# First MLP, first four output tiles: contraction-outermost, between the tiles of the attention's output projection

## The chip, the cores and the metric

One core of one Trainium2 chip. The time is the device time of one execution in microseconds. The median of three runs of the kernel before is 1281.89 us (1281.35 to 1282.48).

## The reference

A trunk of two layers over 512 tokens of width 1024, all in float32. Each layer adds a token mixer, a squared-ReLU MLP and a gated embedding to x; every part starts from an RMS norm of x. The place of this case is the end of the first mixer and the beginning of the first MLP:

```python
x = x + dilated_window_mixer(rmsnorm(x, a_norm[j]), ...)   # ends with  o @ w_o
...
x = x + sq_relu_mlp(rmsnorm(x, mlp_norm[i]), w_up[i], w_down[i])
...
def sq_relu_mlp(h, w_up, w_down):
    return jnp.square(jax.nn.relu(h @ w_up)) @ w_down
```

`w_up` is 1024 x 4096, `w_down` 4096 x 1024.

## The kernel before

x lies transposed, features on the 128 partitions: eight tiles `x[0]` to `x[7]` of 128 features by 512 tokens. A product is float32 made of parts: every operand is split into a rounded high part and the rest (`split`, `fetch`), and `mm3` (L160) issues three matmuls, high by high, low by high and high by low. ACT makes a high part (L169, L172; L137 for weights), DVE the low part (L170, L173; L138 for weights).

The weights lie in one array in the order of `_schedule` (L43). `load` (L141) fetches a block and those ahead of it in that order: one DMA by SyncE (SP, L136), a cast on ACT, a subtraction on DVE. The pool `wp` has three slots each for the raw, high and low blocks of up to 128 x 1024.

`Norm` (L213) collects a norm while x is being made: `tile(m)` splits `x[m]` with the gain and adds its square to `acc` (ACT squares; the additions run on POOL by default and on the engine given to it otherwise, the last one always on DVE, L235). `columns` (L257) sums `acc` over the partitions by matmuls with ones, DVE works out the inverse root, and `row` (L210 and L264) spreads it over all partitions. The scale 1/rms goes on after the matmul (`up`, L640), so matmuls can start on unscaled tiles.

The first mixer's output projection has eight contraction tiles. Six of them (`woA1`) are woven into the last heads; the last two (`woA2`) come behind, one output tile at a time (L616): five matmuls, the residual sum `residual` (L284, DVE), `nM.tile(m)`. Then `mlp(0, nM)` begins: `up(0, b)` makes two hidden tiles by `dense` (L275), each with its eight contraction tiles in a row in one PSUM bank; behind the first come `columns` and, after the second, `row`; DVE and ACT then make relu, scale, square and split of the pair. There are four chunks of eight hidden tiles; `down` of a chunk adds into x. PSUM has eight banks (pool `pp`).

Within each engine the instructions run in the order that a scheduler gave them when the program was built; it keeps close to the order of the code and chooses the slots of the pools.

Of the kernel before, what the change touches and what calls it, by code (L numbers as in the profile page):

```python
# [23 lines left out]
P = 128  # L24
S = 512
D = 1024
KD = D // P
# [12 lines left out]
G_A, G_B, G_MLP, G_PLE, G_FIN, G_Q, G_KV, G_N = 0, 8, 16, 32, 48, 56, 58, 59  # L40


def _schedule():  # L43

    out = []
    for i in range(GH):
        out += [(("qkv", i, b), 1024) for b in range(4)]
        if i == 0:
            out += [(("v0", b), n * 320) for b, n in enumerate((3, 3, 2))]
    out += [(("woA1", m), 768) for m in range(8)]  # L50
    out += [(("woA2", h), 1024) for h in range(2)]
    out += _mlp_blocks(0)
    out += [(("win", b), 832) for b in range(4)]
    out += [((n, 0), c) for n, c in (("uq", 768), ("ukv", 512))]
    for g in range(1, 4):
        out += [((n, g), c) for n, c in (("uq", 768), ("ukv", 512))]
    out += [(("woB", h, b), 1024) for h in range(2) for b in range(4)]
    out += _mlp_blocks(1)
    return out


def _mlp_blocks(l):
    up = lambda c: [(("up", l, c, m), 1024) for m in range(8)]
    down = lambda c: [(("down", l, c, m), 1024) for m in range(8)]
    out = up(0)
    for c in range(NCH):
        if c + 1 < NCH:
            u = up(c + 1)
            out += u[:2] + down(c) + u[2:]
        else:  # L70
            out += down(c)
    out += [(("proj", l, h), 1024) for h in range(2)]
    out += [(("gate", l, m), 1024) for m in range(8)]
    return out
# [3 lines left out]
def trunk(ctx: ExitStack, tc: tile.TileContext, xT, pT, cols, mask, tabs, wts, out):  # L78
    nc = tc.nc
    V, A, G, T = nc.vector, nc.scalar, nc.gpsimd, nc.tensor  # L80
# [14 lines left out]
    def unit(dt=F32, shape=(P, 1024)):  # L95
        return ar.tile(list(shape), dt, tag="u", name=nm("u"))
# [515 lines left out]
        else:  # L612
            weave(attnA(i), woA1(), 48, 7)

    nM = Norm(G_MLP)
    for m in range(KD):  # L616
        ps = bank()
        w = load(("woA2", m // 4))
        c = m % 4 * 256
        mm3(ps, (w[0][:, c:c + P], w[1][:, c:c + P]), oA[4], True, False)  # L620
        T.matmul(ps, w[0][:, c + P:c + 256], oA[7][0], start=False, stop=False)
        T.matmul(ps, w[1][:, c + P:c + 256], oA[7][0], start=False, stop=True)
        residual(m, ps)
        nM.tile(m)


    def mlp(l, nM):
        rb = [None]

        def up(c, b):  # L630
            u = unit()
            ps = []
            for j in range(2):
                ps.append(dense(("up", l, c, 2 * b + j), KD, nM.k))
                if rb[0] is None and j == 0:
                    nM.columns()
            if rb[0] is None:
                rb[0] = nM.row()
            for j in range(2):
                V.scalar_tensor_tensor(u[:, j * S:(j + 1) * S], ps[j], 0.0, rb[0], op0=ALU.max, op1=ALU.mult)  # L640
            A.activation(u, u, AF.Square)
            h, lo = unit(F32R), unit(F32R)
            split(h, lo, u)
            return [(h[:, j * S:(j + 1) * S], lo[:, j * S:(j + 1) * S]) for j in range(2)]

        nG = Norm(G_PLE + 8 * l)
        hid = [up(0, b) for b in range(4)]
        for c in range(NCH):
            flat = sum(hid, [])
            if c == NCH - 1:  # L650
                preload(AF.Sigmoid)
                pr = unit()
                nc.sync.dma_start(out=pr, in_=pT[:, l * 1024:(l + 1) * 1024])
                pe = unit(F32R), unit(F32R)
                split(*pe, pr)
            nxt = []
            if c + 1 < NCH:
                nxt.append(up(c + 1, 0))
            for m in range(KD):
                residual(m, dense(("down", l, c, m), KD, lambda k: flat[k]))  # L660
                if c == NCH - 1:
                    nG.tile(m)
            if c + 1 < NCH:
                nxt += [up(c + 1, b) for b in range(1, 4)]
            hid = nxt
        return nG, pe
# [45 lines left out]
            add(m)  # L712
        return end

    nG, pe = mlp(0, nM)
    nB = Norm(G_B)
    lastA = gate(0, nG, pe, nB)

# [7 lines left out]
    for tp in range(2):  # L726
        ps = [bank(), bank()]
        for k in range(KD):
            w, c = load(("win", k // 2), 1 if tp else 0), (k % 2) * 416
# [19 lines left out]
    for j in range(2):  # L749
        ps = bank()  # L750
# [32 lines left out]
    pk, ps = bank(), bank()  # L783
# [189 lines left out]
    nM = Norm(G_MLP + 8)  # L973
    run(woB(1))
    nG, pe = mlp(1, nM)
# [3 lines left out]
    rb = None  # L979
# [56 lines left out]
    for h in range(2):  # L1036
# [3 lines left out]
        for b in range(4):  # L1040
            ps = [bank() for _ in range(2 if (h, b) == (1, 3) else 1)]
            for j in range(2):
                w = load(("gate", 1, 2 * b + j, h), 1)
# [23 lines left out]
def _arrange(inp):  # L1067
# [18 lines left out]
    def tiles(w, rows, cols_):  # L1086

        a = w[rows][:, cols_]
        return a.reshape(-1, P, a.shape[1]).transpose(1, 0, 2)
# [14 lines left out]
    def block(key):  # L1104
# [18 lines left out]
        if n == "ukv":  # L1123
            kv = ukv[:, key[1] * 512:(key[1] + 1) * 512].reshape(P, 4, 2, 64)
            return kv.transpose(0, 2, 1, 3)
        if n == "up":
            l, c, m = key[1:]
            return one(up[l], 0, 8 * c + m)
# [56 lines left out]
```

## Time and profile before

| | us |
|---|---|
| median of three runs | 1281.89 |
| lowest and highest | 1281.35, 1282.48 |
| the profiled execution's own time | 1284.43 |
| its span in the trace | 1282.6 |
| its mean granted clock of PE | 0.99 of full speed |

The span is the part of the execution that the trace covers. Durations in the rows come from the profiled execution. Starts on PE are the ones to read: a matmul's duration includes its way through the array, and the next one starts before it ends.

### The profile page before, as it was taken

Reading aid. Unit: us, or ns where it says so; the run is one execution under the profiler, and the core shown is the slowest. Engines: PE = TensorE matmul, PEld = TensorE weight load, DVE = VectorE, ACT = ScalarE, POOL = GpSimd, SP = SyncE. Lnnn points to the kernel's source line nnn. Section 1 sums busy time; section 2 is a strip of 40 time slices with the busy share of each in tenths; the row PEclk is TensorE's granted clock in tenths of the full one; section 3 lists DMA queues with packets and bytes.
Section 4 is the critical chain, followed back from the end, with each engine's and each line's share of the span. In section 5 each row is a group of like instructions: output and inputs, shape, how many; then the busy total and the mean of one; then the engine's idle time right before and its main releaser. Section 6 shows DMA issues by size and latency. Waiting matters only on the chain.

```text
span 1282.6 us, 16154 instructions
## 1 busy us (share of the span) xinstructions
PE 1252.5 (98%) x6224; PEld 1057.6 (82%) x6224; DVE 738.5 (58%) x1236; ACT 586.7 (46%) x967; POOL 147.8 (12%) x183
## 2 busy tenths in 40 slices
PE   8999999899999999999999999999999999999997
PEld 6888888688888888888888888888888888888896
DVE  6566676643343343454878999864434434335477
ACT  5566654532231331344558897754313313224464
POOL 5000000300000000021134443220000000000200
PEclk9999999899999999999998999999999999999998
DMA  6111122222222222232221010122232223223242
GB/s 224 66 66 66 58 71 101 68 99 97 92 92 97 99 99 99 99 115 89 81 62 38 17 51 17 50 82 84 98 99 99 99 99 99 98 91 109 98 157 106
DMA packets 34348, 113.18 MB, mean 88 GB/s; under 512 B 4064, under 2 KB 4832, under 8 KB 34272
## 3 DMA queue, kind: packets, MB, share of 16 engines
q1 hardware_dynamic: 34272, 112.15, 26.2%
q8 instruction: 49, 0.80, 0.3%
q14 instruction: 27, 0.22, 0.1%
HBM read 110.04 MB, written 2.10 MB: 87 GB/s over the span
## 4 chain that ended last, share of the span: by engine, by line
PE 85%; DVE 8%; ACT 5%; issue 1%; DMA 1%; DVEq 0%; SPq 0%; ACTq 0%
PE ps L164 26%; PE ps L162 26%; PE ps L163 26%; PE ps L870 2%; DVE wl L138 1%; DVE x L284 1%; PE ps L892 1%; DVE u L173 1%; PE ps L886 1%; DVE u L170 1%; ACT wh L137 1%; ACT h L169 1%; ACT u L169 1%; ACT u L172 1%; PE ps L257 1%
## 5 line engine op out<-in xcount | busy, mean ns | idle before, releaser
L164 PE MATMUL ps<-u,wh 128*128 128x512 f32 (+1 forms) x1256 | 478.0, 381 | 3.4 <-DVE u L173 3.4
L162 PE MATMUL ps<-u,wh 128*128 128x512 f32 (+1 forms) x1256 | 478.1, 381 | 3.0 <-ACT u L172 3.0
L163 PE MATMUL ps<-u,wl 128*128 128x512 f32 (+1 forms) x1256 | 476.9, 380 | 0.0
L137 ACT CAST wh<-wr 128x1024 fp32r<-128x1024 f32 (+4 forms) x213 | 215.4, 1013 | 525.2 <-PE ps L164 454.0
L138 DVE TENSOR_TENSOR wl<-wr,wh 128x1024 fp32r<-128x1024 f32 (+4 forms) x213 | 251.4, 1181 | 97.8 <-ACT wh L137 96.9
L164 PEld LDWEIGHTS ps<-u,wh 128*128 128x128 f32 x1256 | 237.2, 189 | 49.9 <-DVE u L173 5.2
L162 PEld LDWEIGHTS ps<-u,wh 128*128 128x128 f32 x1256 | 237.3, 189 | 47.4 <-ACT u L172 3.5
L163 PEld LDWEIGHTS ps<-u,wl 128*128 128x128 f32 x1256 | 237.2, 189 | 44.2
L284 DVE TENSOR_TENSOR x<-x,ps 128x512 f32<-128x512 f32 x96 | 65.7, 686 | 178.5 <-PE ps L164 178.1
L235 POOL TENSOR_TENSOR h<-h,h 128x512 f32<-128x512 f32 x30 | 48.9, 1631 | 768.5 <-ACT h L234 764.6
L640 DVE SCALAR_TENSOR_TENSOR u<-ps,h 128x512 f32<-128x512 f32 x64 | 44.0, 691 | 135.6 <-PE ps L164 135.6
L162 PE MATMUL ps<-wh,u 128*128 128x512 f32 (+4 forms) x272 | 102.7, 382 | 6.2 <-ACT wh L137 5.5
L170 DVE TENSOR_TENSOR u<-ps,u 128x512 fp32r<-128x512 f32 (+4 forms) x148 | 96.5, 665 | 16.2 <-ACT u L169 14.4
L163 PE MATMUL ps<-wh,u 128*128 128x512 f32 (+4 forms) x272 | 100.0, 370 | 0.0
L164 PE MATMUL ps<-wl,u 128*128 128x512 f32 (+4 forms) x272 | 99.2, 371 | 0.3 <-DVE wl L138 0.3
L169 ACT CAST u<-ps 128x512 fp32r<-128x512 f32 (+3 forms) x148 | 81.7, 572 | 29.8 <-PE ps L510 11.6
L162 PEld LDWEIGHTS ps<-wh,u 128*128 128x128 f32 x272 | 52.2, 192 | 12.2 <-ACT wh L137 5.8
L170 DVE TENSOR_TENSOR u<-u,u 128x1024 fp32r<-128x1024 f32 x34 | 41.7, 1225 | 29.6 <-ACT u L169 29.6
L164 PEld LDWEIGHTS ps<-wl,u 128*128 128x128 f32 x272 | 51.9, 191 | 7.7 <-DVE wl L138 1.3
L163 PEld LDWEIGHTS ps<-wh,u 128*128 128x128 f32 x272 | 52.2, 192 | 6.0 <-DVE u L173 0.3
L863 POOL TENSOR_SCALAR h<-h,sm 128x512 f32<-128x512 f32 x64 | 44.9, 703 | 99.7 <-DVE sm L862 90.9
L870 PE MATMUL ps<-ident,h 128*128 128x128 f32 x256 | 51.0, 272 | 0.3 <-ACT h L856 0.2
(161 smaller groups left out, 1332.3 us busy)
## 6 DMA issues: line engine op xcount, KB each, us to landing
wr<-wts SPq DMA_DIRECT2D x182, 512.0 KB, 3.4
wr<-wts SPq DMA_DIRECT2D x12, 384.0 KB, 3.1
wr<-wts SPq DMA_DIRECT2D x12, 256.0 KB, 4.6
x<-xT SPq DMA_DIRECT2D x8, 256.0 KB, 5.6
wr<-wts SPq DMA_DIRECT2D x4, 416.0 KB, 3.2
out<-u SPq DMA_DIRECT2D x6, 256.0 KB, 2.1
u<-pT SPq DMA_DIRECT2D x2, 512.0 KB, 4.4
wr<-wts SPq DMA_DIRECT2D x2, 480.0 KB, 5.0
```

What stands on the lines that cost most here:

```text
L137: A.copy(hi[:, c], raw[:, c])
L138: V.tensor_tensor(lo[:, c], raw[:, c], fl(hi[:, c]), op=ALU.subtract)
L162: T.matmul(out_, l[0], r[0], start=first, stop=False)
L163: T.matmul(out_, l[1], r[0], start=False, stop=False)
L164: T.matmul(out_, l[0], r[1], start=False, stop=last)
L169: a = A.copy(hi, src)
L170: v = V.tensor_tensor(lo, src, fl(hi), op=ALU.subtract)
L235: (V if self.n == KD - 1 else self.eng).tensor_tensor(self.acc, self.acc, sq, op=ALU.add)
L284: V.tensor_tensor(x[m], x[m], src, op=ALU.add)
L640: V.scalar_tensor_tensor(u[:, j * S:(j + 1) * S], ps[j], 0.0, rb[0], op0=ALU.max, op1=ALU.mult)
L863: return G.tensor_scalar(e, e, rl, 1.0, op0=ALU.mult, op1=ALU.mult)
L870: T.transpose(pt[:, tok(c)], e[:, tok(c)], ident)
```

## The change

After each `woA2` tile from the third on (m > 1), `up_first(m - 2)` multiplies contraction tile m - 2 of the normalised x into four open PSUM banks, one for each of the first four hidden tiles; the last two contraction tiles follow behind the eighth `woA2` tile. The weights of these four hidden tiles come in a new layout: four blocks `upk`, each with two contraction tiles by 512 columns, in place of four blocks of one hidden tile by eight contraction tiles. The order of the weight array has them between the two `woA2` blocks and behind. The norm of this MLP adds its squares on DVE (`Norm(G_MLP, V)`). In `mlp` the column sums, the fifth hidden tile, the row, the output of the first four, and the sixth tile follow each other.

```diff
@@ -48,7 +48,8 @@
         if i == 0:
             out += [(("v0", b), n * 320) for b, n in enumerate((3, 3, 2))]
     out += [(("woA1", m), 768) for m in range(8)]
-    out += [(("woA2", h), 1024) for h in range(2)]
+    out += [(("woA2", 0), 1024), (("upk", 0), 1024), (("woA2", 1), 1024)]
+    out += [(("upk", b), 1024) for b in range(1, 4)]
     out += _mlp_blocks(0)
     out += [(("win", b), 832) for b in range(4)]
     out += [((n, 0), c) for n, c in (("uq", 768), ("ukv", 512))]
@@ -60,7 +61,7 @@
 
 
 def _mlp_blocks(l):
-    up = lambda c: [(("up", l, c, m), 1024) for m in range(8)]
+    up = lambda c: [(("up", l, c, m), 1024) for m in range(4 if (l, c) == (0, 0) else 0, 8)]
     down = lambda c: [(("down", l, c, m), 1024) for m in range(8)]
     out = up(0)
     for c in range(NCH):
@@ -612,7 +613,18 @@
         else:
             weave(attnA(i), woA1(), 48, 7)
 
-    nM = Norm(G_MLP)
+    nM = Norm(G_MLP, V)
+    up0 = []
+
+    def up_first(k):
+
+        w, c = load(("upk", k // 2)), (k % 2) * S
+        if k == 0:
+            up0.extend(bank() for _ in range(4))
+        for j in range(4):
+            cj = slice(c + j * P, c + (j + 1) * P)
+            mm3(up0[j], (w[0][:, cj], w[1][:, cj]), nM.k(k), k == 0, k == KD - 1)
+
     for m in range(KD):
         ps = bank()
         w = load(("woA2", m // 4))
@@ -622,13 +634,16 @@
         T.matmul(ps, w[1][:, c + P:c + 256], oA[7][0], start=False, stop=True)
         residual(m, ps)
         nM.tile(m)
-
-
-    def mlp(l, nM):
+        if m > 1:
+            up_first(m - 2)
+    for k in (KD - 2, KD - 1):
+        up_first(k)
+
+
+    def mlp(l, nM, first=()):
         rb = [None]
 
         def up(c, b):
-            u = unit()
             ps = []
             for j in range(2):
                 ps.append(dense(("up", l, c, 2 * b + j), KD, nM.k))
@@ -636,6 +651,10 @@
                     nM.columns()
             if rb[0] is None:
                 rb[0] = nM.row()
+            return up_out(ps)
+
+        def up_out(ps):
+            u = unit()
             for j in range(2):
                 V.scalar_tensor_tensor(u[:, j * S:(j + 1) * S], ps[j], 0.0, rb[0], op0=ALU.max, op1=ALU.mult)
             A.activation(u, u, AF.Square)
@@ -644,7 +663,15 @@
             return [(h[:, j * S:(j + 1) * S], lo[:, j * S:(j + 1) * S]) for j in range(2)]
 
         nG = Norm(G_PLE + 8 * l)
-        hid = [up(0, b) for b in range(4)]
+        hid = []
+        if first:
+            nM.columns()
+            ps = [dense(("up", l, 0, 4), KD, nM.k)]
+            rb[0] = nM.row()
+            hid += [up_out(first[:2]), up_out(first[2:])]
+            ps.append(dense(("up", l, 0, 5), KD, nM.k))
+            hid.append(up_out(ps))
+        hid += [up(0, b) for b in range(len(hid), 4)]
         for c in range(NCH):
             flat = sum(hid, [])
             if c == NCH - 1:
@@ -712,7 +739,7 @@
             add(m)
         return end
 
-    nG, pe = mlp(0, nM)
+    nG, pe = mlp(0, nM, up0)
     nB = Norm(G_B)
     lastA = gate(0, nG, pe, nB)
 
@@ -1123,6 +1150,8 @@
         if n == "ukv":
             kv = ukv[:, key[1] * 512:(key[1] + 1) * 512].reshape(P, 4, 2, 64)
             return kv.transpose(0, 2, 1, 3)
+        if n == "upk":
+            return tiles(up[0], slice(key[1] * 256, (key[1] + 1) * 256), slice(0, 512))
         if n == "up":
             l, c, m = key[1:]
             return one(up[l], 0, 8 * c + m)
```

PE, from the end of the third `woA2` tile, before (`ps` is the bank written, `u` and `h` the parts of the moving operand, `wh` and `wl` those of the weights; the lines of the change are one to twelve higher):

```order
L164 MATMUL ps394_2256<-h378_2178,wh374_2162 128x512
L621 MATMUL ps394_2256<-h381_2215,wh374_2162 128x512
L622 MATMUL ps394_2256<-h381_2215,wl375_2163 128x512
L162 MATMUL ps398_2270<-h377_2177,wh374_2162 128x512
L163 MATMUL ps398_2270<-h377_2177,wl375_2163 128x512
L164 MATMUL ps398_2270<-h378_2178,wh374_2162 128x512
L621 MATMUL ps398_2270<-h381_2215,wh374_2162 128x512
L622 MATMUL ps398_2270<-h381_2215,wl375_2163 128x512
L162 MATMUL ps400_2282<-h377_2177,wh385_2222 128x512
```

And of the change:

```order
L633 MATMUL ps394_2256<-h381_2215,wh374_2162 128x512
L634 MATMUL ps394_2256<-h381_2215,wl375_2163 128x512
L163 MATMUL ps401_2276<-u390_2239,wh385_2222 128x512
L164 MATMUL ps401_2276<-u390_2239,wl386_2223 128x512
L163 MATMUL ps402_2277<-u390_2239,wh385_2222 128x512
L164 MATMUL ps402_2277<-u390_2239,wl386_2223 128x512
L163 MATMUL ps403_2278<-u390_2239,wh385_2222 128x512
L164 MATMUL ps403_2278<-u390_2239,wl386_2223 128x512
L165 MATMUL ps401_2276<-u391_2240,wh385_2222 128x512
L165 MATMUL ps402_2277<-u391_2240,wh385_2222 128x512
L165 MATMUL ps403_2278<-u391_2240,wh385_2222 128x512
L163 MATMUL ps404_2279<-u390_2239,wh385_2222 128x512
```

Behind the third `woA2` tile (`ps394`) stood the fourth (`ps398`). Now the twelve matmuls of contraction tile 0 (`u390`, `u391`) into four banks (`ps401` to `ps404`) stand there, with the low parts of three of them put behind six high ones.

DVE, from the third residual sum on, before (`x0` to `x3` are pairs of tiles of x, `u` their low parts, L138 a weight split, L284 a residual sum):

```order
L284 TENSOR_TENSOR x1_77<-x1_77,ps394_2256 128x512
L173 SCALAR_TENSOR_TENSOR u391_2240<-x0_76,gains_80,u390_2239 128x512 x2
L284 TENSOR_TENSOR x1_77<-x1_77,ps398_2270 128x512
L173 SCALAR_TENSOR_TENSOR u396_2264<-x1_77,gains_80,u395_2263 128x512
L284 TENSOR_TENSOR x2_78<-x2_78,ps400_2282 128x512
L173 SCALAR_TENSOR_TENSOR u396_2264<-x1_77,gains_80,u395_2263 128x512
L284 TENSOR_TENSOR x2_78<-x2_78,ps407_2302 128x512
L138 TENSOR_TENSOR wl403_2285<-wr401_2283,wh402_2284 128x1024
L173 SCALAR_TENSOR_TENSOR u405_2296<-x2_78,gains_80,u404_2295 128x512 x2
```

And of the change (L285 residual sum, L174 low part, L236 addition of squares, L139 weight split):

```order
L285 TENSOR_TENSOR x1_77<-x1_77,ps394_2256 128x512
L174 SCALAR_TENSOR_TENSOR u391_2240<-x0_76,gains_80,u390_2239 128x512 x2
L236 TENSOR_TENSOR h382_2219<-h382_2219,h393_2253 128x512
L174 SCALAR_TENSOR_TENSOR u396_2264<-x1_77,gains_80,u395_2263 128x512
L236 TENSOR_TENSOR h382_2219<-h382_2219,h397_2267 128x512
L285 TENSOR_TENSOR x1_77<-x1_77,ps405_2292 128x512
L139 TENSOR_TENSOR wl400_2272<-wr398_2270,wh399_2271 128x1024
L174 SCALAR_TENSOR_TENSOR u396_2264<-x1_77,gains_80,u395_2263 128x512
L236 TENSOR_TENSOR h382_2219<-h382_2219,h406_2301 128x512
L139 TENSOR_TENSOR wl410_2319<-wr408_2317,wh409_2318 128x1024
L285 TENSOR_TENSOR x2_78<-x2_78,ps407_2316 128x512
L174 SCALAR_TENSOR_TENSOR u412_2330<-x2_78,gains_80,u411_2329 128x512
```

The additions of squares stand between the low parts, where POOL did them. The split of the second new weight block (`wl400`) stands after the fourth residual sum (`ps405`), before the fourth low part.

ACT, from the second pair of tiles of x on, before (L172 high part, L234 square, L137 weight cast):

```order
L172 ACTIVATE u395_2263<-x1_77,gains_80 128x512
L234 ACTIVATE h397_2267<-x1_77 128x512
L172 ACTIVATE u395_2263<-x1_77,gains_80 128x512
L234 ACTIVATE h399_2279<-x1_77 128x512
L137 CAST wh402_2284<-wr401_2283 128x1024
L172 ACTIVATE u404_2295<-x2_78,gains_80 128x512
L234 ACTIVATE h406_2299<-x2_78 128x512
```

And of the change (L173, L235, L138):

```order
L173 ACTIVATE u395_2263<-x1_77,gains_80 128x512
L235 ACTIVATE h397_2267<-x1_77 128x512
L138 CAST wh399_2271<-wr398_2270 128x1024
L173 ACTIVATE u395_2263<-x1_77,gains_80 128x512
L235 ACTIVATE h406_2301<-x1_77 128x512
L138 CAST wh409_2318<-wr408_2317 128x1024
L173 ACTIVATE u411_2329<-x2_78,gains_80 128x512
```

A weight cast (`wh399`) stands before the fourth high part, where the next cast came two operations later. From the change's lines the number of loads on SP stays the same.

## Rows read from the trace of the kernel before

**Rows 1.** The page's first part: busy us, share of the span and instructions of each engine (PE matmuls, PEld weight loads).
```profile
PE 1252.5 (98%) x6224; PEld 1057.6 (82%) x6224; DVE 738.5 (58%) x1236; ACT 586.7 (46%) x967; POOL 147.8 (12%) x183
```

**Rows 2.** The table by stretch, the whole span cut in three: start and end, length, busy us and instructions of PE, PEld, DVE, ACT and POOL, then the granted clock of PE as a share of full speed, the busy share of the DMA engines and GB/s.
```profile
0.00:219.40 219.40, 209.82 (x1116) 176.38 (x1116) 145.25 (x341) 125.27 (x285) 30.21 (x55) 1.00 0.28 93
219.40:249.90 30.50, 26.25 (x97) 20.44 (x98) 23.20 (x37) 14.82 (x22) 9.81 (x6) 0.83 0.21 69
249.90:1282.60 1032.70, 1016.47 (x5013) 860.83 (x5011) 570.06 (x859) 446.65 (x661) 107.76 (x122) 0.99 0.26 88
```

**Rows 3.** The chain of work that ended last, in order of time, from 219 to 239 us: start us, us, engine, tile written and line. L138 is the split of a weight block, L172 and L173 the high and low parts of a tile of x.
```profile
220.86 1.13 DVE wl L138
...
222.63 0.72 ACT u L172
...
230.87 3.47 DVE u L173 x2
...
235.53 1.13 DVE wl L138
...
236.66 1.68 DVE u L173
...
238.39 0.80 PE ps L164
```

**Rows 4.** The timeline of PE from 218 to 250 us: start us, us, line and operation, out<-in, and in brackets the idle time before it and its releaser. L162 to L164 are the three products of `mm3`, L621 and L622 the other two matmuls of a `woA2` tile, L210 the spread of the row.
```profile
218.79 0.39 PE L164 MATMUL ps<-h,wh 128*128 128x512 f32 x1
...
219.41 0.50 PE L162 MATMUL ps<-h,wh 128*128 128x512 f32 x1 [0.22 <-ACT h L169]
...
219.74 0.39 PE L163 MATMUL ps<-h,wl 128*128 128x512 f32 x1
...
222.72 0.39 PE L622 MATMUL ps<-h,wl 128*128 128x512 f32 x1
...
228.61 0.39 PE L162 MATMUL ps<-u,wh 128*128 128x512 f32 x1
...
231.56 0.39 PE L163 MATMUL ps<-u,wl 128*128 128x512 f32 x1
...
232.69 0.50 PE L164 MATMUL ps<-u,wh 128*128 128x512 f32 x1 [0.75 <-DVE u L173]
...
234.39 0.50 PE L164 MATMUL ps<-u,wh 128*128 128x512 f32 x1 [0.73 <-DVE u L173]
...
235.74 0.50 PE L162 MATMUL ps<-u,wh 128*128 128x512 f32 x1 [0.85 <-ACT u L172]
...
238.39 0.80 PE L164 MATMUL ps<-u,wh 128*128 128x512 f32 x1 [1.92 <-DVE u L173]
...
241.83 0.77 PE L162 MATMUL ps<-u,wh 128*128 128x512 f32 x1
...
247.09 0.42 PE L162 MATMUL ps<-u,wh 128*128 128x512 f32 x1
...
249.88 0.60 PE L210 MATMUL ps<-ident,sm 128*128 128x128 f32 x4
```

**Rows 5.** The table by stretch again, around the pauses; columns as in rows 2.
```profile
231.80:238.40 6.60, 2.35 (x8) 0.98 (x7) 6.60 (x7) 2.38 (x4) 3.33 (x3) 0.89 0.34 100
238.40:242.00 3.60, 3.60 (x13) 3.22 (x14) 1.20 (x2) 1.44 (x2) 0.00 (x0) 0.50 0.27 108
242.00:247.10 5.10, 5.10 (x13) 3.94 (x14) 3.10 (x14) 1.09 (x2) 0.00 (x0) 0.50 0.30 103
```

**Rows 6.** From the timelines of DVE, POOL and ACT around 225 us (start us, us): weight split, residual sums (L284), low parts (L173), additions of squares on POOL (L235), a square (L234) and a weight cast (L137) on ACT; then two lines by source over the whole run (duration in ns, min/median/max); then the page's line for the weight loads (KB each, us to landing).
```profile
220.77 1.22 DVE L138 TENSOR_TENSOR wl<-wr,wh 128x1024 fp32r<-128x1024 f32 x1
...
221.91 1.92 DVE L284 TENSOR_TENSOR x<-x,ps 128x512 f32<-128x512 f32 x3
...
223.75 1.53 DVE L173 SCALAR_TENSOR_TENSOR u<-x,gains,u 128x512 fp32r<-128x512 f32 x2
...
225.09 8.69 POOL L235 TENSOR_TENSOR h<-h,h 128x512 f32<-128x512 f32 x5 [18.25 <-ACT h L234]
...
225.53 0.62 ACT L234 ACTIVATE h<-x 128x512 f32<-128x512 f32 x1
...
227.18 1.04 ACT L137 CAST wh<-wr 128x1024 fp32r<-128x1024 f32 x1
...
L173 DVE SCALAR_TENSOR_TENSOR u<-x,gains,u x48: 737/749/1774, 5.0 to 1212.4; 128x512 fp32r<-128x512 f32 x48
...
L235 DVE TENSOR_TENSOR h<-h,h x12: 678/910/1107, 17.7 to 1213.0; 128x512 f32<-128x512 f32 x12
...
wr<-wts SPq DMA_DIRECT2D x182, 512.0 KB, 3.4
```

**Rows 7.** The first `qkv`, contraction-outermost over four banks: the table by stretch for it, and its first and last matmul at that pace in the timeline of PE.
```profile
11.66:30.06 18.40, 18.40 (x82) 15.20 (x81) 16.10 (x19) 10.71 (x18) 12.92 (x13) 1.00 0.57 202
...
11.66 0.40 PE L164 MATMUL ps<-wl,u 128*128 128x512 f32 x1
...
30.06 0.39 PE L164 MATMUL ps<-wl,u 128*128 128x512 f32 x1
```

**Rows 8.** The timeline of PE at the end of the last norm: the column sums (eight records) and the matmul after them.
```profile
1223.66 0.95 PE L257 MATMUL ps<-ones,h 128*128 128x1 f32 x8
1224.47 0.36 PE L162 MATMUL ps<-u,wh 128*128 128x256 f32 x1
```

## The prediction

> **What bounds the kernel now.** I read the busy time of each engine first [rows 1]: TensorE (PE) is busy 98% of the span, so time can only be won where PE waits or runs slowly. The table by stretch [rows 2] says where that is. Before 219.4 us and after 249.9 us the granted clock is 1.00 and 0.99; in the 30.5 us between them it is 0.83, PE is busy 26.25 us, and VectorE (DVE) 23.20 us. This stretch holds the last part of the first output projection (`woA2`, eight output tiles of 5 matmuls), the first MLP tile, the column sums of the norm and the second MLP tile. The chain of waits [rows 3] runs there through DVE and ScalarE (ACT), not PE: weight split, then the residual sums and splits of x, until PE takes over at 238.39. The timeline of PE [rows 4] shows the wait itself. Up to 231.56 the matmuls follow each other; the first MLP tile needs all eight normalised tiles of x (`nM.k(0)` to `nM.k(7)`), has caught up with DVE, and stands four times, before 232.69, 234.39, 235.74 and 238.39. Behind these pauses the clock goes to its lower level of 1.2 GHz: 0.89 in the stretch with the pauses, then 0.50 up to 247.1 [rows 5].
>
> What the stretch loses, worked out from [rows 4]: from the second matmul of `woA2` (219.74) to the first of the MLP tile (228.61) there are 39 steps, 8.87 us, so 0.2274 us each at full clock. The first step after a wait is 0.33 us (219.41 to 219.74), 0.10 more. The column sums take 0.81 us at full clock [rows 8]. From 219.41 to the spread of the row at 249.88 PE computes 40 + 24 + 24 = 88 matmuls and the column sums: 88 x 0.2274 + 0.10 + 0.81 = 20.92 us. It took 30.47. **The loss is 9.55 us**, of two kinds: 231.56 to 238.39 is 6.83 us for seven steps (1.59), so 5.24 of waiting; 238.39 to 247.09 is 8.70 us for sixteen matmuls and the column sums (4.45), so 4.25 of low clock; 0.06 is left.
>
> **The change, part by part.** *Matmuls.* Their number stays: 4 tiles x 8 contraction tiles x 3 = 96 move forward from the MLP, between the tiles of `woA2`. PE now has 5 + 12 = 17 matmuls for each tile of x, 17 x 0.2274 = 3.87 us, where in `woA2` it had 1.14. The last tile of x is wanted 13 x 0.2274 = 2.96 us or more after the matmuls that make it, since the twelve of k = 5 and of k = 6 stand between.
>
> *DVE.* Each tile of x costs a residual sum (1.92 us for three, 0.64), a split (0.75), one addition of squares and half a weight split (1.22 / 2 = 0.61) [rows 6]. The change moves six additions from GpSimd (POOL) to DVE; the shortest that DVE shows is 0.68 us. Sum 2.68 us, against PE's 3.87: DVE keeps ahead by 1.2 us per tile, so the six additions (4.1 us) are costed at nothing. If PE were not the slower one, they would be on the path. Without POOL's additions the splits should also stay near 0.75: beside POOL's 8.69 us of additions two of them took 3.47 [rows 3, 6]. ACT needs 0.72 + 0.62 for split and square and half of 1.04 for a cast, below 2 us per tile.
>
> *The new wait.* PE is through the third `woA2` tile at 222.72 + 0.23 = 222.95 and comes to k = 0, which needs the high part of the first tile of x. ACT makes it from 222.63, in 0.72 us, to 223.35 [rows 3], in an unchanged order. So PE stands for 0.40 us, 0.45 with the handing over, plus the long first step of 0.10: **0.55 us**. The low part is wanted six matmuls later, at about 224.9; the DVE pair that makes it begins at 223.75 [rows 6] and its first half is done at 224.50. For k = 1 both parts are there by 225.3, and PE comes at 227.4. Bounds of this wait: nothing (if ACT were earlier) and 1.2 us (if the first step waited for the whole DVE pair, 225.28, of which the built order has no sign); I take 0.55, from the rows that make the tile.
>
> *Weights.* The first four MLP tiles come as four contraction-outer blocks of the same 512 KB, one for two contraction tiles, so a block serves 24 matmuls as before; the queue of SyncE has the same number of loads. Three slots each hold raw, high and low parts. In the built order the cast of the second block (`upk` 1) takes the slot that the first `woA2` block leaves after the fourth tile: 227.4, plus cast 1.04 and DVE split 1.22 and handing over, 229.8; PE wants it at 231.2. Spare: 1.4 us. The third and fourth follow slots freed by k = 1 and k = 3, more than 4 us ahead. A load takes 3.4 us to land [rows 6] and its raw slot is free long before. While a DVE split waits for its cast, the residual sum and split of the next tile stand behind it; with this spare they are not late. What is late next, then, is nothing on PE.
>
> *Banks.* PE now goes through four PSUM banks in turn, with a fifth for `woA2`. The same pattern stands at the start of the kernel: from 11.66 to 30.06 the first `qkv` runs contraction-outermost over four banks, 81 steps in 18.40 us, 0.2272 each, at granted clock 1.00 [rows 7]. So I cost it at nothing. The Trainium skill, "TensorE: Matmul & The Clock Gate", section "A second HAM failure mode: psum-queue depth-cycling", speaks against the change: it reports a kernel that cycled through banks, paused briefly between groups, and so had its clock swing between the two levels. By that rule the woven matmuls would run partly at the lower level, and the sum would lose its sign, as the last rival works out; the row above does not bear it out.
>
> *After the weave.* The column sums, the fifth MLP tile, the spread of the row and the sixth tile follow. Four finished tiles wait in banks for the row; with the tiles in work that makes eight banks, as many as there are. PE has three more tiles and two of the next chunk, 5 x 24 x 0.2274 = 27 us, before `down` wants the first of them.
>
> *Sum:* -9.55 + 0.55 = **-9.0 us**. Against the profiled execution, 1284.43 us with a span of 1282.6, that is 1275.4; the median of the runs, 1281.89, is 2.5 lower than that execution, and less 9.0 it is **1272.9 us**. Differences under 0.2% (2.6 us) I count as no change.
>
> **The rivals.** (a) *Late weights.* If a block's slot comes one step later (for `upk` 1 from k = 1, 230.1, then ready at 232.4 against 231.4 for the first use of its low part), PE stands 1.0 us at each of three blocks, with the long first step 3.3 in all: gain 5.7, 1276.2. For it: PE and the casts share three slots, and the second `woA2` block now holds one to the eighth tile. Against: the order above. 11 in 100. (b) *The clock falls all the same*, at the pause before k = 0, and the 4.25 us stay lost: gain 4.75, 1277.2. Against: PE had a pause of 0.62 us from matmul to matmul before 219.41, and nothing slower followed. 3 in 100. (c) *Given back later:* `down` waits for the first four tiles, which are evacuated later than now, by up to the 9 us: 1281.9. Against: the 27 us of cover. 3 in 100. (d) *Slower: the clock falls in the weave.* Small pauses at the changes of bank let the granted clock go to 0.50 there. A matmul at that clock takes (247.09 - 241.83) / 12 = 0.438 us [rows 4], 0.21 more; for all 121 from k = 0 on (96 and five `woA2` tiles) that is 25.5 us, and less the 9.0 it ends 16.5 above, 1298.4. It decides from 9.0 / 0.21 = 43 slow matmuls on. For it: four pauses did this at 232 to 238. Against: [rows 7]. 3 in 100. It is what the Trainium skill's section named above ("TensorE: Matmul & The Clock Gate", on depth-cycling) would make of this kernel. That the change is not carried out as written can be left out: the built order has the weave.
>
> **How the numbers follow.** The forecast has the remaining 80 in 100. Faster by over 0.2%: forecast, (a) and (b), 0.94; within: (c), 0.03; slower: (d), 0.03. The range: at best the whole 9.55 come back and the runs fall at the low side of their spread (1281.35 to 1282.48, half of it 0.6): 1271.7; at worst (a), 1276.2, with a little for the spread. I give 1271.6 to 1276.4, which leaves out (b), (c) and (d).
>
> **What would show it.** In the profile after: granted clock 1.00 from 219 to 258; one gap of PE of about 0.45 us at 223, and none at the three later weight blocks; splits of x at 0.75 and no POOL additions there; the spread of the row at 219.41 + 160 x 0.2274 + 0.2 + 0.45 + 0.81 = 257.3, where the old pace would have it 72 x 0.2274 = 16.4 after 249.88, at 266.3. It is wrong if PE stands for over 2 us between 223 and 252, if the clock there is below 0.95, or if `down` begins with a wait.

## The result, and the profile after

The kernel after takes **1275.78 us** (median of 4 runs, 1275.04 to 1275.94) beside 1282.09 before (4 runs, 1281.35 to 1282.48): ratio 0.9949, 95% interval 0.9937 to 0.9961. It is faster, by 6.3 us where 9.0 were forecast; by the interval 5.0 to 8.1. Two further sets of runs of the same kernel gave 0.9934 and 0.9929, 8.6 and 8.7 us (experiments 1 and 7). The profiled execution took 1275.82 us with a span of 1274.0.

The page's first part and, below it, the table by stretch (columns as in [rows 2]), cut at the start of `woA2`, ahead of k = 0, behind the last woven matmul and behind the spread of the row:

```profile
PE 1246.3 (98%) x6224; PEld 1053.0 (83%) x6224; DVE 738.3 (58%) x1242; ACT 587.6 (46%) x967; POOL 138.4 (11%) x177
```

```profile
0.00:219.40 219.40, 209.56 (x1117) 176.14 (x1117) 145.16 (x341) 125.47 (x285) 30.34 (x55) 1.00 0.28 93
219.40:222.90 3.50, 3.50 (x15) 2.65 (x15) 3.44 (x6) 1.30 (x2) 0.00 (x0) 1.00 0.00 0
222.90:252.00 29.10, 28.80 (x131) 23.91 (x131) 20.04 (x28) 15.32 (x22) 0.00 (x0) 1.00 0.32 109
252.00:260.00 8.00, 8.00 (x38) 6.58 (x37) 4.38 (x16) 3.31 (x5) 0.00 (x0) 1.00 0.20 66
260.00:1274.00 1014.00, 996.47 (x4927) 843.73 (x4925) 565.25 (x855) 442.17 (x656) 108.08 (x122) 0.99 0.26 88
```

PE's busy time fell by 6.2 us against [rows 1] with the same 6224 matmuls: there is less low clock, in which a matmul counts longer, here and at a second place (experiment 1). The stretch that stood at 0.83 [rows 2] is at 1.00 throughout, and in the weave PE is busy 28.80 of 29.10 us. POOL's column is empty there.

The timeline of PE, the rows that answer to [rows 4]: the first matmul of `woA2`, the last of its third tile, k = 0, the column sums, the matmul after them, the spread of the row:

```profile
219.31 0.50 PE L163 MATMUL ps<-h,wh 128*128 128x512 f32 x1 [0.22 <-ACT h L170]
...
222.62 0.39 PE L634 MATMUL ps<-h,wl 128*128 128x512 f32 x1
223.31 0.50 PE L163 MATMUL ps<-u,wh 128*128 128x512 f32 x1 [0.30 <-ACT u L173]
...
250.89 0.95 PE L258 MATMUL ps<-ones,h 128*128 128x1 f32 x8
251.70 0.49 PE L163 MATMUL ps<-u,wh 128*128 128x512 f32 x1
...
257.28 0.60 PE L211 MATMUL ps<-ident,sm 128*128 128x128 f32 x4
```

And PE's waits between 219.4 and 257.3, the whole answer (line that waited, its releaser, us in total, times, longest): the four pauses of [rows 4] are gone and one of 0.3 has come; the 0.2 in front of `woA2` stood there before.

```profile
PE ps L163 <- ACT u L173: 0.3, 1, 0.3
PE ps L163 <- ACT h L170: 0.2, 1, 0.2
```

DVE in the same place answers to [rows 6]: low parts of x (L174) at 0.75 a tile, additions (L236) at 0.68 to 0.69, and the weight split (L139) of the second new block done at 229.65, ahead of PE's k = 2 at 231.17.

```profile
225.70 0.74 DVE L174 SCALAR_TENSOR_TENSOR u<-x,gains,u 128x512 fp32r<-128x512 f32 x1
226.36 0.69 DVE L236 TENSOR_TENSOR h<-h,h 128x512 f32<-128x512 f32 x1
...
228.42 1.23 DVE L139 TENSOR_TENSOR wl<-wr,wh 128x1024 fp32r<-128x1024 f32 x1 [0.22 <-ACT wh L138]
229.56 0.75 DVE L174 SCALAR_TENSOR_TENSOR u<-x,gains,u 128x512 fp32r<-128x512 f32 x1
```

The books of the two profiled executions: up to the spread of the row the kernel after has done 72 matmuls more, 16.37 us at 0.2274.

| | before | after | difference |
|---|---|---|---|
| start of `woA2` | 219.41 | 219.31 | -0.10 |
| from there to the spread | 30.47 + 16.37 | 37.97 | -8.87 |
| from the spread to the end | 1032.72 - 16.37 | 1016.72 | +0.37 |
| span | 1282.6 | 1274.0 | -8.60 |

So between the profiled executions the change is worth 8.6 us. The open question was where the medians of this first set lose 2.3 of it.

### The profile page after: what moved, and what is told of

The parts are those of the page before. It is cut to its first block, busy times and chain, and to the rows that moved or that the text cites. A ratio compares the mean times of both kernels' runs of the same rounds, so it can differ in the third digit from the quotient of the medians.

```text
span 1274.0 us, 16149 instructions
## 1 busy us (share of the span) xinstructions
PE 1246.3 (98%) x6224; PEld 1053.0 (83%) x6224; DVE 738.3 (58%) x1242; ACT 587.6 (46%) x967; POOL 138.4 (11%) x177
## 4 chain that ended last, share of the span: by engine, by line
PE 87%; DVE 6%; ACT 5%; issue 1%; DMA 0%; DVEq 0%; SPq 0%; ACTq 0%
PE ps L165 27%; PE ps L163 27%; PE ps L164 27%; PE ps L897 2%; DVE u L171 1%; ACT u L170 1%; PE ps L919 1%; PE ps L913 1%; DVE wl L139 1%; ACT wh L138 1%; ACT h L170 1%; ACT h L883 1%; DVE sm L882 1%; ACT qk L384 0%; PE ps L258 0%
## 5 line engine op out<-in xcount | busy, mean ns | idle before, releaser
L164 PE MATMUL ps<-u,wl 128*128 128x512 f32 (+1 forms) x1256 | 475.3, 378 | 0.0
L138 ACT CAST wh<-wr 128x1024 fp32r<-128x1024 f32 (+4 forms) x213 | 215.5, 1013 | 512.1 <-PE ps L165 446.7
L139 DVE TENSOR_TENSOR wl<-wr,wh 128x1024 fp32r<-128x1024 f32 (+4 forms) x213 | 250.8, 1178 | 96.3 <-ACT wh L138 95.4
L164 PEld LDWEIGHTS ps<-u,wl 128*128 128x128 f32 x1256 | 236.5, 188 | 44.0
L285 DVE TENSOR_TENSOR x<-x,ps 128x512 f32<-128x512 f32 x96 | 65.7, 686 | 178.5 <-PE ps L165 177.6
L236 POOL TENSOR_TENSOR h<-h,h 128x512 f32<-128x512 f32 x24 | 39.2, 1634 | 769.5 <-ACT h L235 765.9
L164 PE MATMUL ps<-wh,u 128*128 128x512 f32 (+4 forms) x272 | 99.5, 368 | 0.0
L164 PEld LDWEIGHTS ps<-wh,u 128*128 128x128 f32 x272 | 51.8, 190 | 6.0 <-DVE u L174 0.3
```

Source lines behind the costliest of these rows:

```text
L138: A.copy(hi[:, c], raw[:, c])
L139: V.tensor_tensor(lo[:, c], raw[:, c], fl(hi[:, c]), op=ALU.subtract)
L164: T.matmul(out_, l[1], r[0], start=False, stop=False)
L236: (V if self.n == KD - 1 else self.eng).tensor_tensor(self.acc, self.acc, sq, op=ALU.add)
L285: V.tensor_tensor(x[m], x[m], src, op=ALU.add)
```

## The experiments

Every kernel ran beside the kernel before on the same chip. Two theories stood at first. **A:** the gain is where the forecast put it, and the pauses or the low clock of before are not equally long in every execution, those of the profiled one longer. **B:** something behind the stretch gives 2 to 3 us back.

**1. Both kernels again.** No edit.

> The kernel before, unchanged, for a second trace and for its runs one by one. Theory A: the low clock behind the four pauses, and the one near 675 us, do not last equally long in every execution, and the profiled execution of before had long ones; then this trace shows a shorter low-clock time in one of the two places and a span nearer 1280 us than 1282.6, and runs that differ in their mean granted clock. Theory B: the loss of the stretch from 219.4 to 249.9 us is the same in every execution, and the change gives 2 to 3 us back somewhere behind it; then this trace has the spread of the row at 249.9 us again, within 0.3 us, and a span of 1282.6. Ratio of this kernel to before: 1.000 by both.

> The changed kernel, unchanged, for a narrower interval and a second trace. Theory A: 6.0 to 8.6 us faster than before by the runs, spread of the row at 257.2 to 257.4 us, granted clock 1.00 up to there, and span within 1 us of 1274.0. Theory B: the same time, but with a wait or a low-clock time behind 260 us that the traces of before do not have.

Measured: before again 1282.37, ratio 0.9998 (0.9989 to 1.0006); after again **1274.09, ratio 0.9934** (0.9921 to 0.9946), 8.6 us. The ends of the stretch in PE's timeline, first before again, then after again:

```profile
219.06 0.50 PE L162 MATMUL ps<-h,wh 128*128 128x512 f32 x1 [0.22 <-ACT h L169]
...
249.31 0.60 PE L210 MATMUL ps<-ident,sm 128*128 128x128 f32 x4
```

```profile
218.46 0.50 PE L163 MATMUL ps<-h,wh 128*128 128x512 f32 x1 [0.22 <-ACT h L170]
...
256.40 0.60 PE L211 MATMUL ps<-ident,sm 128*128 128x128 f32 x4
```

The stretch takes 30.25 and 37.94: the gain is 30.25 + 16.37 - 37.94 = 8.68. Behind the spread there are 1032.6 us before (span 1281.9) and 1015.9 + 16.37 = 1032.3 after (span 1272.3). Nothing is given back, so B falls. A is not settled by these traces. The stretch of before is nearly as long as in the first profile, but both profiles of before are of executions with a mean granted clock of 0.990, and the runs without a profile differ: of the 58 runs of before on record in these experiments, the 8 at 0.993 took 1280.4 to 1281.5 and the 29 at 0.990 took 1282.1 to 1285.5. So the low clock of before does not last equally long in every execution; at which place it is shorter, no trace shows, and the clock of the first four runs is not on record.

The two executions of the kernel after differ by 1.7 us of span: 0.85 lies ahead of `woA2`, and 0.92 in one wait in front of the second attention. There the rows of the first profile read, on DVE, POOL and PE:

```profile
658.69 0.16 DVE L192 TENSOR_SCALAR sm<-sm 128x4 int32<-128x4 int32 x1
658.88 2.70 DVE L193 TENSOR_SCALAR sm<-sm 128x4 int32<-128x4 int32 x1
```

```profile
658.81 7.25 POOL L820 MEMSET u<- 32x1024 f32 x8
```

```profile
663.83 0.62 PE L814 MATMUL ps<-ident,u 128*128 128x128 f32 x2 [1.76 <-ACT u L789]
```

A step of four numbers per partition takes 2.70 us beside POOL's memsets; in the repeat it takes 1.80 and PE waits 0.84:

```profile
657.99 1.80 DVE L193 TENSOR_SCALAR sm<-sm 128x4 int32<-128x4 int32 x1
```

The two profiles of the kernel before have it at 1.79 and 1.80 in the same place, so it is no price of the change. A third difference between executions is the low clock behind PE's waits in the second attention. The table by stretch there, for before, for the first profile of the change, and for a third one (experiment 7):

```profile
670.00:675.00 5.00, 2.06 (x11) 1.44 (x11) 3.58 (x13) 3.32 (x7) 4.93 (x6) 0.88 0.00 0
675.00:680.00 5.00, 5.00 (x18) 3.54 (x18) 4.45 (x8) 3.14 (x7) 0.00 (x0) 0.50 0.00 0
680.00:685.00 5.00, 5.00 (x27) 4.49 (x27) 4.81 (x8) 3.64 (x8) 0.00 (x0) 0.94 0.00 0
```

```profile
666.40:671.40 5.00, 4.75 (x19) 3.43 (x20) 4.49 (x9) 3.15 (x7) 0.00 (x0) 0.66 0.00 0
```

```profile
665.00:670.00 5.00, 4.37 (x14) 2.96 (x15) 4.49 (x10) 3.17 (x6) 0.79 (x1) 0.59 0.00 0
670.00:675.00 5.00, 5.00 (x23) 4.43 (x23) 4.27 (x7) 3.09 (x7) 0.00 (x0) 0.72 0.01 3
```

By these means (an estimate) PE had half clock there for 6.8, 3.4 and 6.9 us. The same kernel with the same step of 1.80 took 1015.9 us from the spread to the end in the repeat, where the clock is as in the first profile of the change, and 1016.85 (257.05 to 1273.9) in the third.

**2. The additions' engine, with and without the weave.**

```diff
-    nM = Norm(G_MLP)
+    nM = Norm(G_MLP, V)
```

in the kernel before, and the reverse in the kernel after.

> The kernel before with the additions of squares on DVE and nothing else. From the durations of before, DVE's queue from the weight split at 220.86 us has 8 residual sums (0.61 each), 8 splits (0.67), 7 additions (0.60) and three weight splits (1.14): 17.8 us, so the last low part is ready at about 238.7 us, against 238.35 before. By that the pauses stay and the time is the same as before within 1.5 us. The rival, that POOL's additions make DVE late and so the pauses: the last low part is ready 3 us or more earlier, the clock stays at 1.00, and most of the 9.55 us comes back without the weave.

> The changed kernel with the additions of squares on POOL, as before. By the prediction DVE has 1.2 us to spare per tile of x in the weave, so where the additions run costs nothing: the same time as the changed kernel within 0.5 us, spread of the row at 257.3 us, although the splits of x beside a POOL addition take 1.2 to 1.7 us. The rival, that DVE's freedom from POOL is what keeps PE supplied: PE waits at some contraction tiles of the weave, 2 us or more in all, and a part of the gain is gone.

Measured: before with the additions on DVE 1281.54, ratio 0.9990 (0.9981 to 0.9999); after with them on POOL 1274.55, ratio 0.9939 (0.9926 to 0.9951). The first one's PE still stands five times, then at half clock:

```profile
231.44 0.50 PE L164 MATMUL ps<-u,wh 128*128 128x512 f32 x1 [0.37 <-DVE u L173]
232.70 0.50 PE L164 MATMUL ps<-u,wh 128*128 128x512 f32 x1 [0.30 <-DVE u L173]
233.97 0.50 PE L164 MATMUL ps<-u,wh 128*128 128x512 f32 x1 [0.30 <-DVE u L173]
235.92 0.50 PE L162 MATMUL ps<-u,wh 128*128 128x512 f32 x1 [1.45 <-ACT u L172]
236.96 0.50 PE L164 MATMUL ps<-u,wh 128*128 128x512 f32 x1 [0.31 <-DVE u L173]
```

```profile
230.00:236.20 6.20, 3.72 (x12) 1.74 (x11) 6.20 (x11) 4.13 (x8) 0.00 (x0) 1.00 0.04 17
...
237.80:244.60 6.80, 6.80 (x21) 5.64 (x21) 3.09 (x14) 2.28 (x3) 0.00 (x0) 0.50 0.39 137
```

Its low parts take 0.74 to 0.75 each, where beside POOL two took 3.47 [rows 3], and the stretch 29.05 (218.19 to 247.24). It is 1.4 us shorter than in the first profile of before and 1.2 shorter than in the second, so the engine of the additions alone brings little of the 8.9. With the weave the place of the additions changes nothing: the stretch is 37.96 with them on POOL, at clock 1.00.

```profile
219.37 0.50 PE L163 MATMUL ps<-h,wh 128*128 128x512 f32 x1 [0.22 <-ACT h L170]
...
257.33 0.60 PE L211 MATMUL ps<-ident,sm 128*128 128x128 f32 x4
```

One low part ran long beside POOL's additions there, 1.32 us, inside DVE's slack; the others stayed near 0.75:

```profile
225.62 1.32 DVE L174 SCALAR_TENSOR_TENSOR u<-x,gains,u 128x512 fp32r<-128x512 f32 x1 [0.38 <-ACT u L173]
```

**3. What the low clock costs by itself.** The kernel before, with 17 matmuls into a bank that nothing reads put where PE stands in the first MLP tile (`fill` and `pre` by contraction tile):

```diff
+        pre, fill = {6: 4}, {4: 3, 5: 3, 6: 7}
...
+            for _ in range(pre.get(k, 0)):
+                T.matmul(fb, h, rhs(3)[0], start=True, stop=True)
             T.matmul(ps, h, r[0], start=k == 0, stop=False)
             T.matmul(ps, w[1][:, c], r[0], start=False, stop=False)
+            for _ in range(fill.get(k, 0)):
+                T.matmul(fb, h, rhs(3)[0], start=True, stop=True)
```

> The kernel before, with one thing added: in the first MLP tile 17 more matmuls into a bank that nothing reads, put where PE stands and waits for x (3 behind the second product of k = 4, 3 of k = 5, 4 ahead of k = 6 and 7 inside it). They are more work, 17 x 0.2274 = 3.9 us, and make no tile of x earlier. Theory A (two separate losses: 5.2 us of waiting, and 4.25 us of low clock which follows from the waiting): the fillers take the place of the waits, the last part for k = 7 still begins where it did, the granted clock stays at 1.00, and the kernel comes out about 4 us faster than before, 1278.5, with the stretch from the first matmul of woA2 to the spread of the row at about 26.2 instead of 30.4. Rival C (the lower clock does not follow from the pauses but from something else in this stretch): the clock falls to 0.50 as before, the fillers cost up to 3.9 us, and the time is 1282.7 to 1286.6.

Measured: 1279.95, ratio 0.9977 (0.9968 to 0.9987). More work, and faster, by 2.6 us of the medians (1.7 to 4.1 by the interval); the mean granted clock of its 12 runs is 0.994 to 0.996, that of the 17 of before beside them 0.988 to 0.993. The table by stretch at the place of [rows 5], and PE's timeline at the first matmul of `woA2`, the last product for k = 6 and the spread:

```profile
231.60:238.30 6.70, 6.30 (x26) 3.95 (x24) 6.70 (x7) 2.38 (x4) 3.44 (x3) 1.00 0.35 105
238.30:242.00 3.70, 3.63 (x19) 2.87 (x20) 2.38 (x10) 2.40 (x3) 0.00 (x0) 1.00 0.24 94
242.00:247.00 5.00, 5.00 (x26) 4.16 (x25) 1.89 (x7) 0.89 (x2) 0.00 (x0) 1.00 0.33 108
```

```profile
219.29 0.50 PE L162 MATMUL ps<-h,wh 128*128 128x512 f32 x1 [0.22 <-ACT h L169]
...
238.29 0.50 PE L297 MATMUL ps<-u,wh 128*128 128x512 f32 x1 [0.34 <-DVE u L173]
...
246.00 0.60 PE L210 MATMUL ps<-ident,sm 128*128 128x128 f32 x4
```

That product begins at 238.29, as before at 238.39 [rows 4]: x came no earlier. But the clock is 1.00 instead of 0.50, and from there to the spread it takes 7.71 us instead of 11.49. So the pauses bring the low clock, and the low clock costs 3.8 us here, in these two profiles. The expected stretch of 26.2 came out at 26.71, the expected 4 us of gain at 2.6; the interval of the runs holds 3.8.

**4. How much work between the tiles.** Two hidden tiles woven instead of four.

```diff
-        w, c = load(("upk", k // 2)), (k % 2) * S
+        w, c = load(("upk", k // 4)), (k % 4) * 256
...
-        for j in range(4):
+        for j in range(2):
```

> Only the first two MLP tiles are woven instead of four (two blocks of four contraction tiles by 256 columns). PE then has 5 + 6 = 11 matmuls per tile of x, 2.50 us, where DVE has 2.1 to 2.7 us of work per tile. Theory A (the gain is there as long as PE has about as much work per tile of x as DVE needs, and it is lost when PE has much less): nearly no waits beside that for k = 0, granted clock 1.00 or one short low part, time within 1 us of the change with four tiles, 1273.5 to 1275. Rival D (PE has to be clearly slower than DVE, or it catches up): waits of some tenths at several k, the clock falls behind them, and a third or more of the gain goes: 1277 and above.

Measured: 1275.31, ratio 0.9939 (0.9923 to 0.9955). PE's timeline at the end of the weave:

```profile
237.50 0.39 PE L165 MATMUL ps<-u,wh 128*128 128x512 f32 x1
238.97 0.50 PE L163 MATMUL ps<-u,wh 128*128 128x512 f32 x1 [1.09 <-ACT u L173]
```

The clock stays at 1.00 and there are two waits only, for k = 0 as with four tiles and one of 1.24 us (238.97 less 237.50 and 0.23) for the last tile of x, which now has 12 matmuls in front of it and not 24. The stretch of 112 matmuls takes 28.42 (218.41 to 246.83), 2.0 over its 112 x 0.2274 + 0.10 + 0.81 = 26.38; with four tiles it is 37.97 against 37.29, 0.7 over. PE at 2.50 us per tile of x does not catch up with DVE on the way; only the tail is uncovered. The time, 1.2 us over the first repeat of the kernel after, fits, though it was taken on another chip and the intervals overlap.

**5. The wait for k = 0 taken away.** The weave begins one `woA2` tile later.

```diff
-        if m > 1:
-            up_first(m - 2)
-    for k in (KD - 2, KD - 1):
+        if m > 2:
+            up_first(m - 3)
+    for k in (KD - 3, KD - 2, KD - 1):
```

> The change with the weave begun one tile of woA2 later: k = 0 follows the fourth tile of woA2, not the third, and three contraction tiles stand behind the last woA2 tile instead of two. If the wait before k = 0 (0.30 idle, 0.46 against the place that the step could have had) is the only thing left of the loss, it goes: the stretch from the first matmul of woA2 to the spread of the row takes 37.4 to 37.5 us instead of 37.95, and the time is 0.3 to 0.6 us lower than that of the change, about 1273.6. Rival: the block of weights that serves k = 0 is then wanted later and the slots of weights come free later, so a wait at a later block takes the place: stretch 38 us or more, time equal or higher.

Measured: 1273.81, ratio 0.9927 (0.9913 to 0.9941). The table by stretch shows no wait left: PE is busy all of it.

```profile
219.00:222.50 3.50, 3.50 (x15) 2.91 (x16) 3.44 (x6) 1.31 (x2) 0.00 (x0) 1.00 0.00 0
222.50:256.40 33.90, 33.90 (x155) 28.10 (x155) 22.68 (x41) 16.72 (x24) 0.00 (x0) 1.00 0.32 109
```

The stretch is 37.37 (218.99 to 256.36), 0.60 shorter: the wait that the forecast priced at 0.55 was nearly all that was left (160 x 0.2274 + 0.10 + 0.81 = 37.29 is full pace). The expectation's rival, a wait at a later weight block, did not come. The time is too close to that of the change to tell by itself.

**6. The memsets moved.** POOL's eight memsets of 32 x 1024, in the kernel after, to behind the first half of z:

```diff
         rqk.append(r)
+        if tp == 0:
+            kts, qts = ([(unit(F32R), unit(F32R)) for _ in range(2)] for _ in range(2))
+            for t in sum(kts + qts, ()):
+                G.memset(fl(t[QW:]), 0.0)
```

> The change with POOL's eight memsets of 32 x 1024 in front of the second attention moved ahead of its last tile of z, into a place where POOL stands idle for 16 us. In the traces an int32 step of 128 x 4 on DVE that takes 0.16 us elsewhere takes 1.80 us beside these memsets (2.70 in the first profile of the change), on the chain to PE, which then stands 0.84 us (1.76 in that profile). If the memsets are the cause, the step comes back to 0.16 to 0.2 us, PE's wait at that place goes, the low clock behind it too or in part, and the time is 1.6 to 2.6 us lower than that of the change, about 1272. Rival: the step is slow for another reason, or the memsets slow the column sums of the norm ahead of them by as much: no difference, 1273.5 to 1275.

Measured: 1273.01, ratio 0.9922 (0.9908 to 0.9936). The DVE steps, first beside the memsets in their new place (POOL 638.66 to 645.94), then where they stood in the way:

```profile
642.72 0.51 DVE L192 TENSOR_SCALAR sm<-sm 128x4 int32<-128x4 int32 x1
643.26 0.89 DVE L193 TENSOR_SCALAR sm<-sm 128x4 int32<-128x4 int32 x1
...
658.39 0.17 DVE L193 TENSOR_SCALAR sm<-sm 128x4 int32<-128x4 int32 x1
```

The slow step went along with the memsets, to a place where PE does not wait for it, and PE's wait for the transposes is gone. From the spread (256.58) to the end (1271.0) it is 1014.4, against 1015.9 in the repeat and 1016.7 in the first profile of the change. The forecast in the expectation, 1.6 to 2.6, was a little high: 1.1 by the medians, on different chips and with intervals that overlap, 1.5 by the traces. A low part of the clock stays, in the table by stretch:

```profile
665.00:670.00 5.00, 5.00 (x25) 4.46 (x26) 4.45 (x7) 3.92 (x8) 0.00 (x0) 0.67 0.00 0
```

**7. Both edits, and six fillers.** On one chip with the kernel after. The fillers, into an unread bank ahead of the second attention's first K product:

```diff
+    fb = bank()
+    for _ in range(6):
+        T.matmul(fb, qTh[:, :P], qTh[:, S:], start=True, stop=True)
```

> The change as it is, once more, beside the two kernels that follow, so that they can be compared on one chip: 1273.5 to 1275.5, ratio to before 0.993 to 0.995.

> The change with both of the edits that helped: the weave begun one woA2 tile later (0.6 us shorter in its stretch) and POOL's eight memsets ahead of the second attention moved forward (1.5 us shorter behind the spread of the row). They lie 440 us apart and share nothing, so they should add: 2.1 us below the change itself on the same chip, about 1272, ratio to before 0.9915 to 0.993. Rival: PE's wait before the second attention is set by something else at this finer scale, and only one of the two shows: 1273 and above.

> The kernel with both edits and six more matmuls into a bank that nothing reads, in PE's wait of 1.51 us ahead of the first K product of the second attention (behind this wait the granted clock is 0.67 in the five us from 665, about 1.7 us lost there). If a pause of PE is what takes the clock down here as it was in the first MLP, the low part goes and the time falls by up to 1.7 us against the kernel with both edits: about 1270.5. Rival: other short waits around it (0.67, 0.26 and those of the transposes) suffice to take the clock down, and the time stays the same, or rises by some tenths as the fillers take longer than the wait.

Measured, beside before at 1283.38: the kernel after 1274.72, ratio 0.9929 (0.9915 to 0.9942); **both edits 1272.13, 0.9915** (0.9902 to 0.9927); with fillers 1271.40, 0.9905 (0.9891 to 0.9918). Both edits together are 2.6 us below the change by the medians, where 2.1 were expected from their sum; the intervals overlap, and one of the five runs took 1276.01, so the size is not shown by the runs. That the fillers bring anything is not shown either: 0.7 us is inside the intervals. The granted clocks, 0.996 to 0.997 in the four runs with fillers and 0.995 to 0.997 in the five without, point that way, but the profile with both edits has no low clock at that place even without them, though the one with the memsets moved had. With both edits:

```profile
655.00:680.00 25.00, 22.21 (x128) 19.11 (x129) 21.86 (x55) 20.76 (x46) 7.97 (x14) 1.00 0.11 34
```

## Why the prediction was right, and where it was off

**The place and the two kinds of loss** held. The forecast split the 9.55 us into 5.24 of waiting and 4.25 of low clock that follows from it. Experiment 3 took the second away without the first: the clock stayed at 1.00, and 3.8 us came back. The 4.25 was reckoned against full pace without any wait; the difference is a wait of 0.24 for the last addition and some long steps, which stay with the fillers.

**The weave as cause** held: additions on DVE alone shorten the stretch by 1.2 to 1.4 us, the weave with the additions on POOL gives all of it. So the changed engine matters little here. That the six additions cost nothing on DVE held, for the reason given: PE's 3.87 us per tile is the longer one. One count of the prediction is wrong: from the last matmul that makes the last tile of x to the first that uses it are not 13 steps (2.96 us) but 25, with the twelve of k = 5 and the twelve of k = 6 between them: 5.67 us in the trace (242.50 to 248.17). DVE had more room there than the prediction said, and no term of the sum rests on it.

**The new wait**: forecast 0.55 at k = 0, from ACT's high part at 222.63. Measured 0.46 (223.31 against 222.62 + 0.23) and the long step 0.10; with it removed the stretch is 0.60 shorter.

**Weights**: the second block was forecast at 229.8 with 1.4 us to spare, and came at 229.65 for k = 2 at 231.17. Rival (a) did not happen; DVE waited for the casts of the three later blocks, by 0.22 to 1.00, and PE for none of them.

**Banks**: clock 1.00 through all 121 woven matmuls over five banks. The Trainium skill's "TensorE: Matmul & The Clock Gate", section "A second HAM failure mode: psum-queue depth-cycling", tells of a kernel that cycled through banks, idled briefly between groups of matmuls and had its clock swing between the two levels; by that rule the time would have been 1298. The trace shows no such pauses here: beside the one wait for k = 0 there are none between the groups, as there were none in [rows 7]. So the cycling alone did not bring the lower level.

**Given back later**, rival (c): no. From the spread to the end, less the moved matmuls, +0.4 and -0.3 us in two pairs of profiles, and between 257.3 and 640 us the first profile lists no wait of PE.

**The spread of the row** was forecast at 257.3 and stands at 257.28.

**What was off is the first set of runs against the sum.** The sum, -9.0, measured 8.87 and 8.68 in the stretch of two pairs of profiles, and 8.6 and 8.7 in the medians of two repeats. The first set shows 6.3, and 9.0 lies outside its interval (5.0 to 8.1). The prediction took its 9.0 off the median of before and not off the profiled execution; the repeats bear that out. That 1284.43 less 9.0, 1275.4, lies close to the 1275.82 of the profiled execution after proves nothing against that step: 1284.43 is 1.95 above the highest of the first four runs of before, and medians of one kernel differ from set to set, 1274.09 to 1275.78 after and 1282.09 to 1283.38 before. The intervals of the three sets overlap. The traces show three places where executions differ: the time before `woA2` (218.19 to 219.41 over the profiles), DVE's step beside the memsets (0.9 us) and the low clock in the second attention (about 1.0). Whether they, or the chip, make the first set's 2.3 was not measured and stays open. The range reached up to 1276.4 for the sake of rival (a), which did not happen, so that 1275.78 lies in it is in part luck; the mechanism does not rest on it.

## What to carry over

Where PE overtakes the engines that feed it, count what the clock loses behind the pauses beside the pauses themselves: here 3.8 us beside 5.2, and the 3.8 came back even from matmuls that nobody reads. Work that needs the tiles one by one as they are made (contraction outermost, as many banks open as cover the feeding engine's time per tile) removes both; of the two numbers of banks tried, two left a wait of 1.24 us behind the last tile and four left none. Forecast the gain from the books of one profiled execution, take it off the median, and allow for what sets of runs of one kernel differ by, here 1.3 to 1.7 us.

## What had not been expected of the hardware

An int32 step of 128 x 4 on DVE takes 0.16 us alone. Beside POOL's memsets of 0.91 each it takes about the time of one, two or three of them, 0.91 (experiment 4), 1.80 or 2.70, and where it begins inside one, the rest of it, 0.51 (experiment 6). In the second of the two small norms of z this stands on the path to PE and varies from execution to execution. Not every step suffers: in the first profile of the change the nine that follow it beside the same memsets (`tensor_tensor` and `scalar_tensor_tensor`, 661.61 to 663.35) take 0.16 to 0.17 each, and the next `tensor_scalar`, at 663.38, takes 0.90. The Trainium skill, "SBUF — State Buffer", section "Who interferes with whom", has the rule: DVE and GpSimd share a pair of ports, `tensor_scalar` can take both pairs, and whichever of two such instructions comes later is blocked for the whole of the other. The steps of whole memsets agree with it; that two or three memsets go ahead of one step, the section does not say. The same section says that a DVE instruction with two inputs in SBUF contends with GpSimd instructions that read it; the low parts of x agree, 0.75 us alone and up to 1.77 beside POOL's additions [rows 3, 6].
